# Layer 0's feed-forward network on one Trainium2 core: products by Strassen's scheme in PSUM, and the down projection as a phase of its own

## The chip, the core and the metric

The kernel runs on one core of a Trainium2 chip. Its engines work side by side, each through a queue of its own: TensorE (PE, matrix products into the accumulators of PSUM), VectorE (DVE), ScalarE (ACT), GpSimd (POOL), and SyncE (SP), which here issues nearly all transfers from and to memory. The metric is the device time of one execution in microseconds (us). Lower is better.

## The reference, cut to what matters

Two layers (`DEPTH = 2`) work on 512 tokens `x` and, in layer 0, 256 context tokens `h` as well. D_MODEL is 1024, D_FF is 2816.

```python
for l in range(DEPTH):
    ctx_out = l < DEPTH - 1
    mod_x = jnp.split(sc_x @ w_mod[l] + b_mod[l], 6, axis=-1)
    ...
    mx, mc = token_mixers(ux, uc, w_in[l], ...)      # four branches, gates, w_out
    x = x + mod_x[2] * rmsnorm(mx, norm_g[l, 1])
    fx = conv_ffn(modulate(rmsnorm(x, norm_g[l, 2]), mod_x[3], mod_x[4]), ffn_up[l], ffn_conv[l], ffn_down[l])
    x = x + mod_x[5] * rmsnorm(fx, norm_g[l, 3])
    if ctx_out:
        ...

def conv_ffn(u, w_up, w_conv, w_down):
    a = dwconv3(u @ w_up, w_conv)                    # a filter of three taps along the tokens
    gate, val = jnp.split(a, 2, axis=-1)
    return (jax.nn.silu(gate) * val) @ w_down
```

`token_mixers` has an mLSTM, a pooling, a window attention and a short convolution. Each one's output goes through a projection, is weighted with a sigmoid gate, and the four are added ("merge") ahead of `w_out`. The attention's softmax has one more logit per head, the sink.

## The kernel before, in words

**Numbers.** A product of fp32 matrices is made from three products of rounded parts: weight hi by token hi, weight hi by token lo, weight lo by token hi. A weight block (K 1024 x 128 columns, 512 KB) is loaded by SP into a `raw` slot, ACT rounds it to `wh` (L255), and POOL makes `wl = raw - wh` in the slot of `raw` (L256). Slots go round in a fixed ring: 5 of `raw`, 3 of `wh`, more of `raw` in layer 1. The tokens are held as `UH` and `UL`, 8 blocks of 128 features by 768 tokens (512 x, 256 context; layer 1 has 512).

**Order.** The code builds a program which a scheduler then orders for each engine. `run((a, ra), (b, rb))` interleaves generators at the given rates. Every engine runs its instructions in its order, and waits for a semaphore where an operand is not there yet.

**FFN of layer 0.** The 2816 hidden columns are 22 pairs of a gate block and a value block, 128 columns each. `up_pair(f)` makes 2 x 48 matmuls of 384 tokens (8 blocks x 3 passes x 2 halves of the tokens, L301) into a ring of three PSUM tiles `mm, mm, b2`. Then come the filter (`dwconv`: ACT L561, DVE L563 and L566), Silu (ACT L1304), gate times value, and the split into `ah`, `al`. Pairs are taken in groups (`EDGES`), and after a group `down` (L1317) multiplies its activations, which stay in SBUF, with rows of `ffn_down` for six token tiles of 128 and adds the result to `y` (L1343 and after). The last group's `down` is followed, tile by tile, by `residual` (L541 to L556: norm, gain, residual, norm) and `to_u` (L521 to L527: transposes, modulation, new `UH`, `UL` for layer 1).

**Beside it** runs `mod_dve(1, ch)` for six channels: layer 1's modulation, a product of one row with 1024 x 1024 weights. DVE makes it from `mraw` tiles (512 KB each, two buffers) with 32 multiply-adds of 512 columns (L427) a channel where both x and context need it (channels 1 and 0), 16 elsewhere.

**Elsewhere.** In a merge, the product (`mm`) times `bth` goes to SBUF (DVE L1026) and is added to `acc` (L1027). After the last merge ACT L1254 and DVE L1255 split `acc` into `UH` and `UL` for the `w_out` products (L1270). In the attention each softmax has scores (PE L750, L754), mask and maximum (L761), exp with its sum `den` (ACT L767), the sink's exp (ACT L769), their sum (DVE L770), the reciprocal (L771) and the scaling (L772); transposes follow (L795), and products with the values (L782).

Of the kernel before, what the change touches and what calls it, by code (L numbers as in the profile page):

```python
# [17 lines left out]
P = 128  # L18
# [6 lines left out]
EDGES = ((0, 3, 6, 9, 12, 15, 17, 22), (0, 4, 8, 12, 15, 18, 22))  # L25
DOWN_ROWS = (5, 4)
DOWN_AHEAD = (2, 1)
# [17 lines left out]
def block_kernel(  # L45
# [148 lines left out]
    ps_ = {"mm": 2, "b2": 1, "b1": 2, "pool": tc.alloc_tile_pool(name="psum", bufs=1, space=PSUM)}  # L194

    def pst(tag, w):
        return ps_["pool"].tile([P, w], F32, tag=tag, name=nm(tag), bufs=ps_[tag])
# [209 lines left out]
    def mod_dve(l, ch, md):  # L407
# [104 lines left out]
    def to_u(np_, l, which, j0, xns, ks=range(KC)):  # L512
# [5 lines left out]
        for k in ks:  # L518
            ps = b1()
            for i, xn in enumerate(xns):  # L520
                PE.transpose(ps[:, i * P : (i + 1) * P], xn[:, k * P : (k + 1) * P], ident)  # L521
            tt = np_.tile([P, n], F32, tag="tt", name=nm("tt"), bufs=3)
            ACT.activation(
                tt, ps[:, 0:n], AF.Identity, scale=a[:, k, part : part + 1], bias=b[:, k, part : part + 1]
            )
            DVE.tensor_copy(UH[:, k, o : o + n], tt)  # L526
            DVE.tensor_sub(UL[:, k, o : o + n], tt, UH[:, k, o : o + n].bitcast(F32))  # L527
            yield
# [155 lines left out]
    def attention(l, ap, pools, kept, ys, pc, sk, mid):  # L684
# [37 lines left out]
        for jq in range(4):  # L722
# [10 lines left out]
            for i in range(6 if hc else 4):  # L733
                pt = bp.tile([P, 2, 640], F32, tag="pt", name=nm("pt"), bufs=2)
# [8 lines left out]
                w = len(kts) * P  # L743
                for hd in range(2):
                    h = 2 * jq + hd
# [25 lines left out]
                    DVE.reciprocal(den, den)  # L771
                    DVE.tensor_scalar(pt[:, hd, 0:w], pt[:, hd, 0:w], den, None, op0=ALU.mult)  # L772
                    if next(av_part, 0) is None:
                        yield
                def finish(i=i, jq=jq, g=g, kts=kts, pt=pt):
# [3 lines left out]
                    def times(k0, kk, ph, pl):  # L779
                        for a, kt in enumerate(kk):  # L780
                            for r in (ph, pl):
# [204 lines left out]
    def gate_tile(l, nb, f, p, stops=()):  # L986
# [4 lines left out]
        th = p.tile([P, T], F32, tag="th", name=nm("bth"), bufs=2 if l == 0 else 4)  # L991
# [14 lines left out]
    def merge(l, nb, ys, acc, ct, first, kept):  # L1006
        hc = l == 0
        n = T if hc else TX
        yh, yl = ({p: y and y[q] for p, y in ys.items()} for q in range(2))
        for f in range(8):  # L1010
            if kept:
                th = ct.tile([P, T], F32, tag="th", name=nm("bth"), bufs=2 if hc else 4)
# [8 lines left out]
            pb = wide(mm(), hc)  # L1021
            proj(pb, bw[0], bw[1], yh, yl, 4, lambda i: i * 256 + ff * P, even(hc))
            if first:
                DVE.scalar_tensor_tensor(acc[f][:, 0:n], th[:, 0:n], 1.0, pb[:, 0:n], op0=ALU.add, op1=ALU.mult)
# [24 lines left out]
    def pool_branch(l, ys, pc, ct):  # L1049
# [3 lines left out]
        for g in range(4):  # L1053
# [17 lines left out]
            iv = ct.tile([P, T], F32, tag="th", name=nm("iv"), bufs=2 if hc else 4)  # L1071
            nc.sync.dma_start(iv, k_pinv[g].partition_broadcast(P))
# [38 lines left out]


# [363 lines left out]
```

## Time and profile before

| | |
|---|---|
| three runs, median (lowest to highest) | 2670.55 us (2669.33 to 2674.66) |
| the profiled execution: device time | 2671.79 us |
| its span in the trace | 2670.1 us |
| mean granted TensorE clock | 0.992 of full speed |
| moved over the span | 297.96 MB, mean 112 GB/s |
| layer 0 FFN in the span, from its first products to layer 1's first | 1020.09 to 1600.67 us |

The span is what the trace covers, from the first instruction to the last. Busy time of PE counts overlapping matmuls, so a difference between starts of equal matmuls is the better measure of what one takes. In the rows below `L301` is a line of the kernel, `out<-in` are names of the program, `x16` is a count, and `[1.17 <-ACT wh L255]` is idle time ahead of the first instruction of a group and what ended it. "PEld" is TensorE's loading of weights, which lies beside its products.

### The profile page before, as it was taken

Reading aid. Unit: us, or ns where it says so; the run is one execution under the profiler, and the core shown is the slowest. Engines: PE = TensorE matmul, PEld = TensorE weight load, DVE = VectorE, ACT = ScalarE, POOL = GpSimd, SP = SyncE. Lnnn points to the kernel's source line nnn. Section 1 sums busy time; section 2 is a strip of 40 time slices with the busy share of each in tenths; the row PEclk is TensorE's granted clock in tenths of the full one; section 3 lists DMA queues with packets and bytes.
Section 4 is the critical chain, followed back from the end, with each engine's and each line's share of the span. In section 5 each row is a group of like instructions: output and inputs, shape, how many; then the busy total and the mean of one; then the engine's idle time right before and its main releaser. Section 6 shows DMA issues by size and latency. Waiting matters only on the chain. (4 is left out here: it accounts for less than half of the span.)

```text
span 2670.1 us, 35624 instructions
## 1 busy us (share of the span) xinstructions
PE 2577.0 (97%) x13859; PEld 2302.0 (86%) x13859; DVE 1444.8 (54%) x2510; ACT 991.5 (37%) x1663; POOL 896.8 (34%) x522
## 2 busy tenths in 40 slices
PE   6999999999999999999999999999999999999998
PEld 2988999999999979989999978778888877888886
DVE  6688784333462546577656565665434636523334
ACT  3454553222222334323322345555232333543332
POOL 3222223333232323333332333323343443444432
PEclk9999999999999999999999999999999999999999
DMA  6334353322332433233433342323433436433321
GB/s 231 91 111 127 109 158 122 108 80 64 102 93 65 135 128 120 87 110 119 134 121 101 126 136 80 111 81 117 127 106 98 121 96 189 150 95 95 101 64 56
DMA packets 321267, 297.96 MB, mean 112 GB/s; under 512 B 12532, under 2 KB 264252, under 8 KB 321100
## 3 DMA queue, kind: packets, MB, share of 16 engines
q1 hardware_dynamic: 320184, 294.11, 35.9%
q8 instruction: 110, 1.80, 0.3%
q10 hardware_dynamic: 916, 1.58, 0.2%
q14 instruction: 57, 0.47, 0.1%
HBM read 269.30 MB, written 26.35 MB: 111 GB/s over the span
## 5 line engine op out<-in xcount | busy, mean ns | idle before, releaser
L256 POOL TENSOR_TENSOR wl<-raw,wh 128x1024 fp32r<-128x1024 f32 x260 | 636.9, 2452 | 1189.7 <-ACT wh L255 1150.3
L301 PE MATMUL mm<-UH,wh 128*128 128x384 f32 (+2 forms) x2248 | 652.1, 350 | 8.5 <-DVE UH L526 4.8
L301 PE MATMUL mm<-UL,wh 128*128 128x384 f32 (+2 forms) x2248 | 642.4, 347 | 1.8 <-DVE UL L527 1.8
L255 ACT CAST wh<-raw 128x1024 fp32r<-128x1024 f32 x260 | 272.8, 1050 | 535.7 <-PE mm L301 359.8
L301 PE MATMUL mm<-UH,wl 128*128 128x384 f32 (+2 forms) x2248 | 449.1, 346 | 0.0
L301 PEld LDWEIGHTS mm<-UH,wh 128*128 128x128 f32 x2248 | 409.3, 189 | 31.7 <-DVE UH L526 5.7
L301 PEld LDWEIGHTS mm<-UL,wh 128*128 128x128 f32 x2248 | 411.9, 189 | 22.5 <-DVE UL L527 2.2
L301 PEld LDWEIGHTS mm<-UH,wl 128*128 128x128 f32 x2248 | 392.2, 188 | 21.3 <-issue 3.3
L427 DVE SCALAR_TENSOR_TENSOR macc<-mraw,sc,macc 128x512 f32<-128x512 f32 x224 | 204.6, 938 | 20.7 <-DMA mraw<-in_w_mod_dram 19.7
L301 PE MATMUL mm<-ys,wh 128*128 128x384 f32 (+1 forms) x768 | 168.6, 366 | 8.7 <-DVE bth L1026 8.1
L1238 POOL TENSOR_TENSOR wrl<-raw,wrh 128x1024 fp32r<-128x1024 f32 x48 | 119.1, 2494 | 168.9 <-ACT wrh L1237 126.4
L301 PEld LDWEIGHTS mm<-ys,wh 128*128 128x128 f32 x768 | 137.6, 191 | 21.1 <-DVE bth L1026 5.2
L563 DVE SCALAR_TENSOR_TENSOR fcv<-mm,fcol,fcv 128x511 f32<-128x511 f32 x89 | 58.3, 655 | 136.6 <-ACT fcv L561 136.5
L1237 ACT CAST wrh<-raw 128x1024 fp32r<-128x1024 f32 x60 | 62.7, 1051 | 142.7 <-DMA raw<-in_ffn_down_dram 69.2
L301 PE MATMUL mm<-U,wh 128*128 128x512 f32 (+1 forms) x496 | 111.2, 377 | 0.1
L301 PEld LDWEIGHTS mm<-U,wh 128*128 128x128 f32 x496 | 89.2, 188 | 17.2 <-DVE y L545 0.3
L1026 DVE SCALAR_TENSOR_TENSOR bth<-bth,mm 128x768 f32<-128x768 f32 (+1 forms) x48 | 39.2, 818 | 113.6 <-PE mm L301 106.1
L1317 PE MATMUL mm<-wrh,ah 128*128 128x512 f32 x302 | 95.6, 393 | 1.1 <-DVE fcv L566 1.1
L1317 PE MATMUL mm<-wrl,ah 128*128 128x512 f32 x302 | 95.5, 393 | 0.0
L1317 PE MATMUL mm<-wrh,al 128*128 128x512 f32 x302 | 95.5, 393 | 0.0
L301 PE MATMUL mm<-ys,wl 128*128 128x384 f32 (+1 forms) x384 | 86.1, 360 | 0.0
L563 DVE SCALAR_TENSOR_TENSOR cv<-mm,pcol,cv 128x511 f32<-128x511 f32 (+1 forms) x28 | 17.7, 632 | 116.9 <-ACT cv L561 116.9
(306 smaller groups left out, 4138.0 us busy)
## 6 DMA issues: line engine op xcount, KB each, us to landing
raw<-in_w_in_dram SPq DMA_DIRECT2D x140, 512.0 KB
mraw<-in_w_mod_dram SPq DMA_DIRECT2D x88, 512.0 KB
raw<-in_ffn_up_dram SPq DMA_DIRECT2D x88, 512.0 KB
raw<-in_ffn_down_dram SPq DMA_DIRECT2D x44, 512.0 KB
raw<-in_w_branch_dram SPq DMA_DIRECT2D x32, 512.0 KB
gates<-bth SPq DMA_DIRECT2D x24, 384.0 KB
bth<-gates SPq DMA_DIRECT2D x24, 384.0 KB
raw<-in_w_out_dram SPq DMA_DIRECT2D x16, 512.0 KB
```

Of the source, the lines that this page charges most:

```text
L255: ACT.copy(h, raw)
L256: POOL.tensor_sub(lo, raw, h.bitcast(F32))
L301: PE.matmul(ps[:, c0:c1], lhsT=lw, rhs=r, start=s, stop=e)
L427: DVE.scalar_tensor_tensor(acc[v], mr[:, kk], sc[:, k, v : v + 1], acc[v], op0=ALU.mult, op1=ALU.add)
L563: DVE.scalar_tensor_tensor(dst[:, a + 1 : b], src[:, a : b - 1], w[0], dst[:, a + 1 : b], op0=ALU.mult, op1=ALU.add)
L1026: DVE.scalar_tensor_tensor(th[:, 0:n], th[:, 0:n], 1.0, pb[:, 0:n], op0=ALU.add, op1=ALU.mult)
L1237: ACT.copy(h, raw)
L1238: eng.tensor_sub(lo, raw, h.bitcast(F32))
L1317: PE.matmul(ps[:, h], lhsT=av[i][q][:, j * P : (j + 1) * P], rhs=ws[i][r][:, h], start=pi == 0 and i == 0, stop=pi == 2 and i == len(av) - 1,)
```

## The change

**Up products.** The first three pairs (`PLAIN`) stay as they were. Each of the other 19 is a product of a 2 x 2 block matrix of weights (gate and value block by two halves of K, 512 each) with a 2 x 2 block matrix of tokens (two halves of K by two halves of the tokens, 384 each). It is made from 7 block products (Winograd's form of Strassen's scheme) of 12 matmuls in place of 8 of 12. The weights are combined for each pair (`s12` on DVE, `s34` on POOL), the tokens once (`T1` to `T4`). Partial sums stay in PSUM half `v0`, from which ACT takes copies `p1`, `u1`, `u2` as it grows. A pair's last two products (`rest`) come after the next pair's first. Seven `raw` and six `wh` slots are lent for this phase, which make 12 and 9. The activations go to memory (`a_d`, 393 KB a pair), in fp32.

**Down** follows when all pairs are done: two sweeps of three token tiles, each over all 22 pairs, accumulating in three PSUM tiles. Each sweep loads and splits all of `ffn_down` and reads its half of `a_d`. The matmuls of `down` remain as many as before.

**Modulation.** Channels 1 and 0 run beside the sweeps at rate 0.35, channels 2, 4, 3 and 5 beside layer 1's heads at rate 0.4 with one `mraw` buffer in place of two.

**Merges and attention.** The product is weighted and added in its PSUM tile. The last merge uses the ring `mm, mm, b2` and writes `UH`, `UL` itself. The sink is one more column under the exp; the two heads of a tile share a reciprocal.

The diff, cut to its core:

```diff
+PLAIN = 3
+LAST_DOWN = 4
+RATE_MOD1 = 0.4
...
+        def conv_act(f, g, v):
...
+            ACT.activation(g[:, 0:T], cg, AF.Silu)
+            DVE.tensor_mul(cv, g[:, 0:T], cv)
+            nc.sync.dma_start(a_d[f], cv)
...
+        def prepare(f):
...
+            DVE.tensor_add(s12[:, lo], r2[:, lo], r2[:, hi])
+            DVE.tensor_sub(s12[:, hi], s12[:, lo], r1[:, lo])
+            POOL.tensor_sub(s34[:, lo], r1[:, lo], r2[:, lo])
+            POOL.tensor_sub(s34[:, hi], r1[:, hi], s12[:, hi])
+            got = part(r1, o1), part(s12, os12), part(s34, os34)
...
+            ACT.copy(h, r2[:, hi])
+            POOL.tensor_sub(l_, r2[:, hi], h.bitcast(F32))
...
+        for j in range(3):
...
+            DVE.tensor_sub(t1, blocks(j + 3, 0), blocks(j, 0))
...
+        def pair(f, weights):
...
+            product(v0, w1, 0, "11", True, True)
+            ACT.copy(p1, v0)
+            if pend:
+                pend.pop()()
+            product(g0, w1, 512, "21", True, True)
+            product(v0, w12, 512, "T2", False, True)
+            ACT.copy(u1, v0)
+            product(g1, w12, 0, "T1", True, True)
+            product(v0, w34, 0, "T3", False, True)
+            ACT.copy(u2, v0)
+            DVE.tensor_add(v1, g1, u2)
+            def rest():
+                product(v0, w22, 0, "T4", False, True)
+                product(g1, w34, 512, "22", False, True)
+                DVE.tensor_add(g0, g0, p1)
+                DVE.tensor_add(g1, g1, u1)
+                conv_act(f, g, v)
...
+        def factors(s, f):
+            w = split(load(ffn_down[0][f * P : (f + 1) * P, :].unsqueeze(1), 1))
...
+            nc.sync.dma_start(af, a_d[f, :, s * HT : (s + 1) * HT])
+            ACT.copy(ah, af)
+            (DVE, POOL)[f % 2].tensor_sub(al, af, ah.bitcast(F32))
...
+        run((sweeps(), 1), (seq(*[mod_dve(1, ch, mp) for ch in (1, 0)]), 0.35))
...
-                DVE.scalar_tensor_tensor(th[:, 0:n], th[:, 0:n], 1.0, pb[:, 0:n], op0=ALU.add, op1=ALU.mult)
-                DVE.tensor_add(acc[f][:, 0:n], acc[f][:, 0:n], th[:, 0:n])
+                DVE.scalar_tensor_tensor(pb, th[:, 0:n], 1.0, pb, op0=ALU.add, op1=ALU.mult)
+                DVE.tensor_add(pb if last else acc[f][:, 0:n], acc[f][:, 0:n], pb)
+            if last:
+                ACT.activation(UH[:, f, 0:n], pb, AF.Copy, scale=0.5)
...
-                    es = small("es", 1, 4)
-                    ACT.activation(es, sk[:, h : h + 1], AF.Exp, bias=negm)
-                    DVE.tensor_add(den, den, es)
...
+        mods1 = seq(*[mod_dve(1, ch, dp, 1) for ch in (2, 4, 3, 5)]) if l == 1 else iter(())
+        run((heads(), 1), (fills(), 1), (mods1, RATE_MOD1))
...
-            run((up, 1), (seq(*[mod_dve(1, ch, fp) for ch in (1, 0, 2, 4, 3, 5)]), 1))
```

The order on the engines moves with it, at three places that matter below. First, ScalarE in the middle of the up products. Before, one cast of weights (`wh`) stood between the steps of the filter (`fcv`), the modulation (`mh`) and the activations (`ah`):

```order
L255 CAST wh_2572_11090<-raw_2571_11088 128x1024
L1308 CAST ah_2536_2537_10979<-fcv_2534_2535_10971 128x768
L255 CAST wh_2610_11374<-raw_2609_11372 128x1024
L561 ACTIVATE fcv_2569_2570_11082<-mm_2568_11033,fcol_2016_8329 128x768
L436 CAST mh_2599_11303<-macc_2582_2583_11165 128x512
L1304 ACTIVATE fcv_2569_2570_11082<-fcv_2569_2570_11082 128x768
L255 CAST wh_2626_11450<-raw_2625_11448 128x1024
```

Now one pair's row of eleven instructions is this, from its copy `u2` to the next pair's `u2`. The tiles `v_2409` and `mm_2408` are of one pair, `v_2433` is the next one's; `raw_2445` is the value block of the pair after those in work:

```order
L1269 COPY u2_2414_2415_10563<-v_2409_10560 128x384
L1261 COPY p1_2434_2435_10697<-v_2433_10696 128x384
L593 ACTIVATE cv_2440_2441_10739<-v_2409_10560,fcol_1946_8165 128x768
L593 ACTIVATE cg_2442_2443_10745<-mm_2408_10559,fcol_1946_8165 128x768
L1197 CAST wh_2454_10827<-raw_2445_10807 128x512
L1266 COPY u1_2436_2437_10698<-v_2433_10696 128x384
L1179 CAST wh_2450_10819<-s12_2446_10809 128x1024
L1179 CAST wh_2452_10823<-s34_2447_10810 128x1024
L1171 ACTIVATE mm_2408_10559<-cg_2442_2443_10745 128x768
L1179 CAST wh_2472_10951<-raw_2468_10941 128x1024
L1269 COPY u2_2438_2439_10699<-v_2433_10696 128x384
```

Three casts of 1024 columns and one of 512 stand between copies that PE's next products need, where two stood for a pair before.

Second, GpSimd at the same place: of one pair, `s34` in two halves (L1193, L1194), and the low parts of its four weights:

```order
L1193 TENSOR_TENSOR s34_2447_10810<-raw_2444_10805,raw_2445_10807 128x512
L1198 TENSOR_TENSOR wl_2455_10828<-raw_2445_10807,wh_2454_10827 128x512
L1194 TENSOR_TENSOR s34_2447_10810<-raw_2444_10805,s12_2446_10809 128x512
L1180 TENSOR_TENSOR wl_2449_10816<-raw_2444_10805,wh_2448_10815 128x1024
L1180 TENSOR_TENSOR wl_2451_10820<-s12_2446_10809,wh_2450_10819 128x1024
L1180 TENSOR_TENSOR wl_2453_10824<-s34_2447_10810,wh_2452_10823 128x1024
```

Before, there were two of 1024 columns for a pair (L256) and the down weights' (L1238). Three of 512 were added, and one of 1024.

Third, TensorE where the products of `up` end and those of `down` begin. Before, each group of pairs was followed by its `down` with weights `wrh`, `wrl` and activations `ah`, `al` from SBUF:

```order
L301 MATMUL mm_2363_9879<-UL_3_59,wh_2361_9875 128x384 x2
L301 MATMUL mm_2363_9879<-UH_2_58,wl_2362_9876 128x384 x16
L1317 MATMUL b2_2378_9954<-wrh_2340_2341_9796,ah_2307_2308_9589 128x512 x2
L1317 MATMUL b2_2378_9954<-wrl_2342_2343_9797,ah_2307_2308_9589 128x512 x2
L1317 MATMUL b2_2378_9954<-wrh_2340_2341_9796,al_2309_2310_9590 128x512 x2
```

Now it happens once, behind the last pair's last product, and `ah_2688` comes from memory:

```order
L1244 MATMUL mm_2660_12029<-UL_3_59,wh_2644_11911 128x384
L1244 MATMUL mm_2660_12029<-UH_2_58,wl_2645_11912 128x384 x4
L1312 MATMUL mm_2681_12188<-wh_2685_12193,ah_2688_12198 128x512 x2
L1312 MATMUL mm_2681_12188<-wl_2686_12194,ah_2688_12198 128x512 x2
L1312 MATMUL mm_2681_12188<-wh_2685_12193,al_2689_12199 128x512 x2
```

The first two `ah` lie in space that held `UH` and `UL` (`spare` in the code), which the product ahead of them still reads.

## Rows read from the trace of the kernel before

**Rows 1.** Page: each engine's busy us, share of the span, instructions.

```profile
PE 2577.0 (97%) x13859; PEld 2302.0 (86%) x13859; DVE 1444.8 (54%) x2510; ACT 991.5 (37%) x1663; POOL 896.8 (34%) x522
```

**Rows 2.** Windows: stretch, length, busy us of PE PEld DVE ACT POOL, clock, DMA share, GB/s.

```profile
0.00:50.00 50.00, 32.36 (x92) 12.95 (x93) 32.73 (x49) 15.34 (x23) 12.81 (x25) 0.93 0.89 298
943.00:951.00 8.00, 4.24 (x13) 3.17 (x12) 7.45 (x10) 1.43 (x4) 2.78 (x2) 0.79 0.57 172
1049.00:1550.00 501.00, 497.13 (x2679) 464.48 (x2678) 309.11 (x368) 154.00 (x182) 177.79 (x78) 1.00 0.37 115
1890.00:2150.00 260.00, 255.89 (x1325) 220.92 (x1324) 127.00 (x264) 81.22 (x124) 103.33 (x62) 1.00 0.39 113
2215.00:2250.00 35.00, 30.09 (x110) 23.30 (x110) 33.16 (x37) 14.85 (x25) 17.05 (x8) 0.85 0.76 227
```

**Rows 3.** Timeline of PE: first products of two neighbouring blocks of columns.

```profile
1049.14 0.52 PE L301 MATMUL mm<-UH,wh 128*128 128x384 f32 x2
...
1057.47 0.51 PE L301 MATMUL mm<-UH,wh 128*128 128x384 f32 x2
```

**Rows 4.** Chain that ended last: 24 matmuls of 512 columns in `down`.

```profile
2359.30 5.48 PE b L1317 x24
```

**Rows 5.** ScalarE's groups by line and form: busy, mean ns, idle before.

```profile
L255 ACT CAST wh<-raw 128x1024 fp32r<-128x1024 f32 x260 | 272.8, 1050 | 535.7 <-PE mm L301 359.8 <-issue 81.5 <-DMA raw<-in_ffn_up_dram 47.8
L1304 ACT ACTIVATE fcv<-fcv 128x768 f32<-128x768 f32 x22 | 18.6, 843 | 25.3 <-DVE fcv L566 25.3
L811 ACT COPY avl<-b 64x256 f32<-64x256 f32 x40 | 14.8, 369 | 22.4 <-PE b L782 21.7
L1058 ACT COPY pd<-mm 128x512 f32<-128x512 f32 x8 | 4.7, 585 | 9.2 <-PE mm L301 8.5 <-DVE hb L959 0.8
```

**Rows 6.** VectorE's groups by line and form.

```profile
L427 DVE SCALAR_TENSOR_TENSOR macc<-mraw,sc,macc 128x512 f32<-128x512 f32 x224 | 204.6, 938 | 20.7 <-DMA mraw<-in_w_mod_dram 19.7
L545 DVE TENSOR_TENSOR y<-y,gt 128x512 f32<-128x512 f32 x20 | 13.3, 688 | 8.1 <-ACT sq L503 4.9 <-DMA gt<-gdram 3.2
L902 DVE TENSOR_TENSOR E<-b,E 128x384 f32<-128x384 f32 x24 | 12.0, 551 | 9.0 <-PE b L892 9.0
```

**Rows 7.** GpSimd's groups by line and form.

```profile
L256 POOL TENSOR_TENSOR wl<-raw,wh 128x1024 fp32r<-128x1024 f32 x260 | 636.9, 2452 | 1189.7 <-ACT wh L255 1150.3 <-issue 23.5 <-DVE den L771 8.9
L437 POOL TENSOR_TENSOR ml<-macc,mh 128x512 fp32r<-128x512 f32 x32 | 41.6, 1313 | 103.5 <-ACT mh L436 86.6 <-DVE yr L814 9.7 <-DVE pt L772 5.2
```

**Rows 8.** Timeline: three loads of 512 KB tiles, issue and first use.

```profile
1068.87 5.80 SPq L262 DMA_DIRECT2D raw<-in_ffn_up_dram  x3
...
1074.35 1.04 ACT L255 CAST wh<-raw 128x1024 fp32r<-128x1024 f32 x1 [6.45 <-DMA raw<-in_ffn_up_dram]
...
1117.60 2.52 SPq L415 DMA_DIRECT2D mraw<-in_w_mod_dram  x2
...
1121.22 0.75 DVE L427 SCALAR_TENSOR_TENSOR macc<-mraw,sc,macc 128x512 f32<-128x512 f32 x1 [1.49 <-DMA mraw<-in_w_mod_dram]
...
1204.55 0.34 SPq L262 DMA_DIRECT2D raw<-in_ffn_down_dram  x1
...
1208.62 1.05 ACT L1237 CAST wrh<-raw 128x1024 fp32r<-128x1024 f32 x1 [3.16 <-DMA raw<-in_ffn_down_dram]
```

**Rows 9.** Timeline, 1209.5 to 1210.5: GpSimd and VectorE side by side.

```profile
1209.75 2.39 POOL L1238 TENSOR_TENSOR wrl<-raw,wrh 128x1024 fp32r<-128x1024 f32 x1 [4.28 <-ACT wrh L1237]
...
1210.31 2.38 DVE L427 SCALAR_TENSOR_TENSOR macc<-mraw,sc,macc 128x512 f32<-128x512 f32 x1
```

**Rows 10.** Timeline of PE where the two layers' last merges end.

```profile
947.23 1.22 PE L1270 MATMUL mm<-wrh,UH 128*128 128x512 f32 x2 [3.76 <-DVE bth L1026]
...
2240.19 1.12 PE L301 MATMUL mm<-ys,wh 128*128 128x512 f32 x3 [2.12 <-DVE bth L1026]
```

**Rows 11.** Waits of PE: total us, times, longest us.

```profile
PE b L521 <- ACT y L555: 9.3, 5, 2.6
...
PE b L782 <- DVE pl L804: 4.5, 4, 1.8
```

More of the change, by code (lines that the diff above doesn't have):

```diff
@@ L192, in more_slots, with __init__, back, psum @@
             slots["raw"].append(arena.base + 4 * arena.take(1024)[0])
-    ps_ = {"mm": 2, "b2": 1, "b1": 2, "pool": tc.alloc_tile_pool(name="psum", bufs=1, space=PSUM)}
+    class Lent:
+        def __init__(self, **counts):
+            self.got = []
+            for kind, n in counts.items():
+                for _ in range(n):
+                    piece = arena.take(1024)
+                    off = arena.base + 4 * piece[0]
+                    slots[kind].insert(0, off)
+                    self.got.append((kind, off, piece))
+        def back(self):
+            for kind, off, piece in self.got:
+                slots[kind].remove(off)
+                arena.give(*piece)
+    cuts = []
+    def psum(**tags):
+        cuts.append((tags, tc.alloc_tile_pool(name=nm("psum"), bufs=1, space=PSUM)))
+    psum(mm=2)
+    psum(b2=1, b1=2)
     def pst(tag, w):
-        return ps_["pool"].tile([P, w], F32, tag=tag, name=nm(tag), bufs=ps_[tag])
+        tags, pl = next(c for c in cuts if tag in c[0])
+        return pl.tile([P, w], F32, tag=tag, name=nm(tag), bufs=tags[tag])
     def mm():
@@ L1004, in early_gates, with merge @@
                 yield
-    def merge(l, nb, ys, acc, ct, first, kept):
+    def merge(l, nb, ys, acc, ct, first, kept, last=False):
         hc = l == 0
+        places = cycle((mm, mm, b2) if last else (mm,))
         n = T if hc else TX
@@ L1113, in xsrc, with make_rows, rows @@
+    def make_rows():
+        def rows(wr, w, k, bufs, eng=POOL):
+            raw, _ = load(w[k * P : (k + 1) * P, :].unsqueeze(1), 1)
+            h = wr.tile([P, 1024], F32R, tag="wrh", name=nm("wrh"), bufs=bufs)
+            lo = wr.tile([P, 1024], F32R, tag="wrl", name=nm("wrl"), bufs=bufs)
+            ACT.copy(h, raw)
+            eng.tensor_sub(lo, raw, h.bitcast(F32))
+            return h, lo
+        return rows
     def xsrc(l, j):
@@ L1231, in block_kernel @@
         wr = Pool()
-        def rows(wr, w, k, bufs, eng=POOL):
-            raw, _ = load(w[k * P : (k + 1) * P, :].unsqueeze(1), 1)
-            h = wr.tile([P, 1024], F32R, tag="wrh", name=nm("wrh"), bufs=bufs)
-            lo = wr.tile([P, 1024], F32R, tag="wrl", name=nm("wrl"), bufs=bufs)
-            ACT.copy(h, raw)
-            eng.tensor_sub(lo, raw, h.bitcast(F32))
-            return h, lo
+        rows = make_rows()
         fc = conv_params(l)
         ws = []
-        for k, _ in enumerate(merge(l, 0, y4, acc, mg, False, True)):
+        if not hc:
+            UH, UL = (at("U1", [P, KC, TX], F32R, base + 4 * KC * TX * i) for i in range(2))
+            arena.give(-(RAW + WH) * 1024 - 2 * KC * TC, 2 * KC * TC)
+        for k, _ in enumerate(merge(l, 0, y4, acc, mg, False, True, True)):
             if k < 6:
@@ L1347, in ffn @@
             ffn.last = (pairs[lo:hi], ws)
-        if l == 0:
-            pcs[1] = params(1, nc.sync)
-            up = ffn()
-            for _ in range(2):
-                next(up)
-            run((up, 1), (seq(*[mod_dve(1, ch, fp) for ch in (1, 0, 2, 4, 3, 5)]), 1))
-        else:
-            run((ffn(), 1))
+        run((ffn(), 1))
         fp.release()
```

276 lines of the change are left out of this document (215 added, 61 removed).

## The prediction

> **What bounds the kernel now.** The page's first part comes first [rows 1]: TensorE is busy for 97% of the span, every other engine for little more than half of it or less. The windows then say whether this holds where the change is made [rows 2]: over 501 us in the middle of layer 0's feed-forward network (FFN) PE is busy for 497.1 us at the full granted clock (1.00), while DVE has 309 us of work, ACT 154 and POOL 178, and the transfers run at 115 GB/s. So this stage lasts as long as its matmuls do, and fewer matmuls shorten it, if nothing else becomes as long. PE's timeline prices them: two neighbouring blocks of 48 matmuls of 384 columns start at 1049.14 and 1057.47 [rows 3], so one takes 8.33 / 48 = 0.1735 us and a block product of 12 takes 2.08. A matmul of 512 columns in `down` takes 5.48 / 24 = 0.228 us [rows 4].
>
> What has to be found out is whether the other engines keep pace with 7 products a pair (84 x 0.1735 = 14.57 us, before 96 x 0.1735 = 16.66), and what the new order costs at its seams.
>
> **A, the products.** 19 pairs x 12 matmuls x 0.1735 = -39.6 us. `down` keeps its 22 x 6 x 3 x 2 = 792 matmuls, 792 x 0.228 = 181 us, before and after.
>
> **B, the ring of one pair.** By sums the other engines have room in 14.57 us. ACT: three casts of 1.05, one of half the width, Silu 0.84, two filter steps of Silu's width and three copies of 0.48 [rows 5], some 8 us. POOL: three of 2.45 and three of 1.31 [rows 7], 11.3 us. But the order closes a ring. `v0` is one accumulator: each copy of it (`u1`, `u2`) must be done before the next product adds to it. ACT's row in the order shows `u2` behind the casts of weights for a later pair, and these wait for a load into the slot that product T4 of the pair in work sets free (12 `raw` slots, four a pair, so three pairs round). Followed once round: T4 2.08; load, the mean of two lone ones, 3.62 and 4.07 [rows 8], 3.85; POOL's first half of `s34` 1.31 (512 columns, as L437 [rows 7]); DVE's first half of `s12` 0.69 (as L545 [rows 6]); ACT's half cast 0.59 (as L1058, 512 columns [rows 5]); POOL's low part of it 1.31 and second half of `s34` 1.31; ACT's cast of `s34` 1.05, Silu 0.84, the next cast 1.05 [rows 5]; `u2` 0.48 (384 columns, between 0.369 for 256 and 0.585 for 512 [rows 5]); DVE's add of `v1` 0.55 (as L902 [rows 6]); then T4 again. The sum is 15.11 us. A hand-over between engines takes some 0.08 us (a cast that starts at 1208.62 and lasts 1.05 is followed by POOL at 1209.75 [rows 8, 9]), and eight of them would add 0.6, though ends on one engine overlap the next start. I take 15.3, so B = 19 x (15.3 - 14.57) = +14. From below it is 0 (the ring has slack). From above the load takes 5.5 us, as behind two others [rows 8], the ring 16.8 to 16.95, and B = +45.
>
> In that ring DVE's `s12` starts only when POOL's `s34` has ended, although neither needs the other. I put it so because the trace has such a case: a DVE multiply-add that begins at 1210.31 beside a POOL subtraction (1209.75, 2.39 us) lasts 2.38 us [rows 9], where the mean is 0.94 [rows 6]. Without the hold `s12` lies beside `s34`, the sum is 14.42, below PE's 14.57, and B falls to 0 or a little more.
>
> The Trainium skill (page "SBUF — State Buffer", section "Who interferes with whom") makes this a rule that speaks against the change: a VectorE instruction with two inputs in SBUF and a GpSimd one that reads SBUF share a pair of ports, and the later one stands still until the earlier has ended. By it the ring is as I have put it, without it the phase would come out 14 us shorter. The trace agrees in the case named.
>
> **C, the start of the phase, +6 (2 to 14).** The first copies `p1` stand behind POOL's two halves of `s34` and a cast: 2 x 1.31 + 1.05 + 0.48 = 4.15 us, of which one product covers 2.08, so 2.1 are left. While three pairs run plainly, the ring of PSUM has two tiles in place of three (the rest goes to `v`), so a product waits for the filter of the one two before: four steps of 768 columns on ACT and DVE, some 3.4 us at Silu's 0.84 each [rows 5] (an estimate), part of it covered. The 12 subtractions that make T1 to T4 are 12 x 0.69 = 8.3 us of DVE between the filters of these pairs; hidden, or all of it open: that is the upper end.
>
> **D, from up to down, +5 (2 to 10).** The first `ah` lie in space of `UH` and `UL`, so their load can start only when the last product has read it, and PE waits for a load (3.62 [rows 8]) and a cast (0.48): 4.1 us. When PE last waited that long, at 947, the clock granted over those 8 us was 0.79 in the mean [rows 2, 10]; as much again costs 8 x 0.21 = 1.7. The load is of 197 KB in place of 512 and may land sooner.
>
> **E, the end of the layer, -4 (-8 to +3).** Before, transposes in the tail waited 9.3 us in five waits for the normalised `y` [rows 11]. Now three of the six tiles are finished a sweep earlier, and only the last two waits stay. Against it stands the change of sweeps: the same three PSUM tiles are read by ACT and DVE before the second sweep writes them.
>
> **F, merges, -4 (-9 to +3).** `w_out` waits 3.76 us at 947 behind the last merge and its pass over `acc`, with 1.7 us of clock, and PE waits 2.12 at 2240 [rows 2, 10]. DVE's and ACT's pass now lies inside the merge, over three PSUM tiles in turn. The last block's chain (two DVE steps, ACT, DVE) stays open. In the window from 2215 DVE is busy 33.2 of 35 us [rows 2], so work saved there shows.
>
> **G, attention, -3 (-8 to +3).** One ACT and one DVE instruction less per head and tile, and all high products ahead of the low ones: the waits for `pl` were 4.5 us in four [rows 11]. The first head's scaling now waits for the second.
>
> **H, modulation in layer 1, +3 (0 to +10).** 64 multiply-adds x 0.938 = 60 us of DVE [rows 6] go into about 260 us in which DVE is busy for 127 and PE idle for 4.1 [rows 2]. There is room, but DVE's order can hold a mask or a filter behind a modulation step that waits for its load: with one buffer each of 32 loads is waited for, 1.49 us where two buffers did it before [rows 8], 48 us in all if none of it is covered (the scenario below).
>
> **I, the sweeps themselves, +4 (0 to +15).** For each f PE has 18 matmuls, 4.1 us. POOL has 2.45 and half of the activations' low parts, about 2.9. DVE has 60 us of modulation in 181. Transfers: 44 x (524 + 197 KB) + 16 x 524 KB = 40.1 MB in about 185 us, 217 GB/s. POOL and DVE together would have 130 + 60 + 12 = 202 us if they never overlapped; where they hold each other as in [rows 9], this is the term that grows.
>
> **Sum:** -39.6 + 14 + 6 + 5 - 4 - 4 - 3 + 3 + 4 = -18.6. The profiled execution has a span of 2670.1, and 2671.79 as device time, 1.7 around it; the median of the runs is 1.2 lower than that. So 2670.1 - 18.6 + 1.7 - 1.2 = 2652 us.
>
> **The rivals.** A difference under 0.2% (5.3 us) is about what a measurement of this kernel cannot tell from none.
>
> 1. *As summed:* 2652, its own range 2638 to 2664 (B from 0.3 to 1.2 us a pair, the seams at either half of their bounds). Chance 0.62.
> 2. *PE alone sets the pace of the pairs* (no hold on `s12`, or a load in under 3.5 us): B = 0, and -32.6 in all, 2638. The rows that speak for it are 3.62 as a landing at 512 KB, and that the sum is only 0.5 us over PE's; against it is the hold in [rows 9]. With quiet seams it reaches 2628. Chance 0.16.
> 3. *Loads land late:* where a load comes behind the write of `a_d` and another load, 5.5 us [rows 8], the ring is 16.8, as long as the old pair, B = +43, 2681. For it: at 1068 three loads queue so. Against: in the order each load of the ring stands alone behind a write that has been ready for long. Chance 0.08.
> 4. *The other side, down becomes bound by transfers:* the sweeps want 217 GB/s where this stage had 115 [rows 2]. At 157 GB/s, 40.1 MB would take 255 us in place of 188: +67, 2719. It decides below about 200 GB/s. Against it the trace shows 298 GB/s in the first 50 us and 227 from 2215 on, with the DMA engines busy 0.89 and 0.76 [rows 2]. Chance 0.05.
> 5. *Modulation holds DVE in layer 1:* the 48 us of H uncovered in place of 3: 2697. Against it: with two buffers, such loads held DVE for 19.7 us over all 224 steps of the kernel [rows 6]. Chance 0.05.
>
> The remaining 0.04 is a mixture of late seams that ends within 5 us of before. Faster by over 0.2%, below 2665: nearly all of 1, all of 2 and part of the rest, 0.80. Slower: 3, 4, 5 with less than all of their price at times, 0.14. The range of 8 in 10 takes 1 with both of its flanks and 2: 2630 to 2670.
>
> **What would show it.** In the changed profile: starts of the first product of successive pairs 15.3 us apart (14.6 means rival 2, 16.8 rival 3); idle time of PE before T4, ended by DVE `v1`, of about 0.7 us a pair; DVE's `s12` starting as POOL's `s34` ends, or lasting 1.3 us and more; one wait of about 4 us before the first `down` product, and a clock under 1.0 behind it; the sweeps at 4.1 us for each f with a rate near 215 GB/s (6 us and 150 GB/s means rival 4); layer 1 as long as before within 5 us. The prediction is wrong if the pairs are at 14.6 and the seams add nothing, or if PE waits in the sweeps for weights (`wl`) that POOL has not split in time.

## The result, and the profile after

The changed kernel takes 2702.7 us (median of five runs, 2699.3 to 2708.1) against 2670.7 before: a ratio of 1.0119, 95% interval 1.0105 to 1.0134, slower by some 32 us. Forecast were 2652 us, 2630 to 2670. The profiled execution is the longest of the five, with 2708.07 us and a span of 2706.3.

The page's first part, to be read beside [rows 1]: TensorE is busy for 10 us less, GpSimd for 207 us more, and the span is 36.2 us longer. TensorE's 228 matmuls fewer are 39.6 us at 0.1735 us each, so some 30 us of that gain went into products that took longer (the granted clock was 0.982 in the mean, 0.992 before), and its idle time grew from 93 to 139 us. Waits are paid twice here, as idle time and as a slower clock behind it: after the wait of 3.2 us ahead of `down`, the granted clock was 0.50 of full speed from 1382.0 to 1387.3.

```profile
PE 2567.0 (95%) x13631; PEld 2280.4 (84%) x13631; DVE 1445.6 (53%) x2478; ACT 1053.1 (39%) x1696; POOL 1104.0 (41%) x644
```

Four windows of the changed kernel, cut at events that both traces have: three plain pairs, 19 pairs of the scheme, the two sweeps of `down`, and layer 1 from its first gates to its `w_out`. Columns as in [rows 2].

```profile
1015.47:1082.68 67.21, 57.81 (x378) 57.11 (x377) 42.14 (x63) 33.24 (x43) 43.02 (x21) 0.92 0.21 64
1082.68:1382.01 299.33, 282.60 (x1598) 275.94 (x1597) 165.51 (x262) 140.52 (x190) 207.79 (x109) 1.00 0.34 109
1382.01:1601.46 219.45, 200.43 (x842) 158.88 (x843) 133.02 (x133) 84.07 (x141) 145.13 (x89) 0.94 0.56 186
1679.38:2279.32 599.94, 568.41 (x2871) 474.95 (x2871) 348.51 (x666) 230.28 (x389) 216.01 (x114) 0.98 0.46 137
```

The stretch of layer 1 in the kernel before, between the same two events, is a row of its own:

```profile
1670.16:2244.64 574.48, 555.77 (x2821) 468.89 (x2821) 306.53 (x633) 229.17 (x412) 209.53 (x108) 0.99 0.40 117
```

So: up to the FFN's first product the kernel is 4.6 us ahead (1015.47 against 1020.09). From there to layer 1's first gates it takes 663.9 in place of 650.1 us, +13.8. Layer 1 then takes 599.9 in place of 574.5, +25.5, with 42 us more work on VectorE, and the rest +1.5. The 299.33 - 3.4 = 295.9 us of the scheme (its last product ends 3.4 us ahead of the window's end) are 20.6 less than 19 x 16.66; the three plain pairs take 67.2 where 6 x 8.33 = 50 and some transposes would do; the sweeps take 219 where their products need 181.

Inside the scheme, the list of TensorE's waits from 1085 to 1376 and its timeline at two neighbouring pairs:

```profile
PE v L1244 <- DVE v L1270: 11.9, 17, 1.2
```

```profile
1127.78 0.44 PE L1244 MATMUL v<-th,wh 128*128 128x384 f32 x1 [0.66 <-DVE v L1270]
1143.22 0.44 PE L1244 MATMUL v<-th,wh 128*128 128x384 f32 x1 [0.58 <-DVE v L1270]
```

These pairs follow at 15.44 us, and T4 waits for `v1` in 17 of the 19 pairs: the ring of the forecast. The other engines' timeline shows it as written there. VectorE's first half of `s12` starts beside GpSimd's first half of `s34` and lasts 1.46 us, where such a step takes 0.69 [rows 6]; at the end come the cast of `s34` behind POOL, Silu, the next cast, the copy `u2` and the add `v1`.

```profile
1133.91 1.29 POOL L1193 TENSOR_TENSOR s<-raw,raw 128x512 f32<-128x512 f32 x1 [2.76 <-DMA raw<-in_ffn_up_dram]
...
1134.29 1.46 DVE L1191 TENSOR_TENSOR s<-raw 128x512 f32<-128x512 f32 x1
...
1139.46 1.06 ACT L1179 CAST wh<-s 128x1024 fp32r<-128x1024 f32 x1 [1.36 <-POOL s L1194]
...
1140.41 0.81 ACT L1171 ACTIVATE mm<-cg 128x768 f32<-128x768 f32 x1
1141.16 1.04 ACT L1179 CAST wh<-raw 128x1024 fp32r<-128x1024 f32 x1
...
1142.10 0.47 ACT L1269 COPY u<-v 128x384 f32<-128x384 f32 x1
...
1142.60 0.57 DVE L1270 TENSOR_TENSOR v<-mm,u 128x384 f32<-128x384 f32 x1 [0.39 <-ACT u L1269]
```

In the sweeps, VectorE and GpSimd from 1460 on, and then the change of sweeps, where TensorE waits for VectorE's reading of the first PSUM tile (L577), which stands behind two multiply-adds of the modulation:

```profile
1460.90 5.20 POOL L284 TENSOR_TENSOR wl<-raw,wh 128x1024 fp32r<-128x1024 f32 x2
1463.85 9.82 DVE L455 SCALAR_TENSOR_TENSOR macc<-mraw,sc,macc 128x512 f32<-128x512 f32 x4 [2.36 <-DMA mraw<-in_w_mod_dram]
1466.06 1.46 POOL L1306 TENSOR_TENSOR al<-af,ah 128x384 fp32r<-128x384 f32 x1
1467.48 5.64 POOL L284 TENSOR_TENSOR wl<-raw,wh 128x1024 fp32r<-128x1024 f32 x2
...
1487.87 4.26 DVE L455 SCALAR_TENSOR_TENSOR macc<-mraw,sc,macc 128x512 f32<-128x512 f32 x2
...
1492.06 0.68 DVE L577 TENSOR_TENSOR y<-mm,gt 128x512 f32<-128x512 f32 x1
...
1494.24 1.22 PE L1312 MATMUL mm<-wh,ah 128*128 128x512 f32 x2 [4.51 <-DVE y L577]
```

A multiply-add takes 2.45 us at 1463.85, in step with GpSimd's subtractions, where one that nothing holds takes 0.75; the mean of the 56 in the sweeps is 1.30 us. TensorE's waits in the sweeps (1360 to 1600) are for the modulation's two matmuls (L467) and for this change:

```profile
PE b L467 <- ACT mh L464: 8.8, 3, 5.3
PE mm L1312 <- DVE y L577: 5.4, 2, 4.5
PE b L467 <- POOL ml L465: 3.5, 5, 1.0
PE mm L1312 <- ACT ah L1305: 3.2, 1, 3.2
```

The wait for `ah` ends where the sweeps' window begins. The other three and two shorter ones come to the 19 us in which TensorE is idle there. With the clock at 0.94 of full speed over 219 us (13 us) and 50 small matmuls of the modulation and of transposes (some 6 us, an estimate from their columns), they account for the 38 us. In layer 1 (1679 to 2279), VectorE's waits for the modulation's loads:

```profile
DVE macc L455 <- DMA mraw<-in_w_mod_dram: 45.9, 18, 5.3
DVE macc L453 <- DMA mraw<-in_w_mod_dram: 20.9, 6, 7.7
```

### The profile page after: what moved, and what is told of

Its sections match the earlier page's. It is cut to its first block, busy times and chain, and to the rows that moved or that the text cites. A ratio compares the mean times of both kernels' runs of the same rounds, so it can differ in the third digit from the quotient of the medians.

```text
span 2706.3 us, 35636 instructions
## 1 busy us (share of the span) xinstructions
PE 2567.0 (95%) x13631; PEld 2280.4 (84%) x13631; DVE 1445.6 (53%) x2478; ACT 1053.1 (39%) x1696; POOL 1104.0 (41%) x644
## 5 line engine op out<-in xcount | busy, mean ns | idle before, releaser
L329 PE MATMUL mm<-UH,wh 128*128 128x384 f32 (+2 forms) x1848 | 554.8, 356 | 14.4 <-DVE cv L598 8.0
L329 PE MATMUL mm<-UL,wh 128*128 128x384 f32 (+2 forms) x1848 | 545.6, 352 | 1.8 <-DVE UL L559 1.8
L329 PE MATMUL mm<-UH,wl 128*128 128x384 f32 (+2 forms) x1848 | 377.0, 350 | 0.0
L329 PEld LDWEIGHTS mm<-UH,wh 128*128 128x128 f32 x1848 | 341.3, 191 | 36.9 <-issue 10.5
L329 PEld LDWEIGHTS mm<-UL,wh 128*128 128x128 f32 x1848 | 343.4, 191 | 23.1 <-DVE UL L559 2.2
L329 PEld LDWEIGHTS mm<-UH,wl 128*128 128x128 f32 x1848 | 324.6, 189 | 21.2 <-issue 2.8
L1244 PE MATMUL v<-th,wh 128*128 128x384 f32 x228 | 78.5, 344 | 13.5 <-DVE v L1270 11.9
L1180 POOL TENSOR_TENSOR wl<-s,wh 128x1024 fp32r<-128x1024 f32 x38 | 90.0, 2395 | 0.0
L1244 PE MATMUL v<-tl,wh 128*128 128x384 f32 x228 | 76.4, 335 | 0.0
L802 ACT ACTIVATE pt<-pt,negm 128x513 f32<-128x513 f32 (+2 forms) x80 | 58.1, 727 | 33.9 <-DVE negm L799 33.4
```

The costliest lines, as they stand in the source:

```text
L329: PE.matmul(ps[:, c0:c1], lhsT=lw, rhs=r, start=s, stop=e)
L802: ACT.activation(pt[:, hd, 0 : w + 1], pt[:, hd, 0 : w + 1], AF.Exp, bias=negm, accum_out=den[:, hd : hd + 1])
L1180: POOL.tensor_sub(lo, src, h.bitcast(F32))
L1244: PE.matmul(ps, lhsT=w[r][:, o + k * P : o + (k + 1) * P], rhs=B[b][q][:, k], start=start and i == 0, stop=stop and i == 11, skip_group_ch ...
```

## The experiments

Theory: the 50 us that the forecast missed are VectorE's, which stands still in three places (in layer 1 for loads into one buffer; in the sweeps, and where the pairs of the scheme are made, behind GpSimd), with work in its order that TensorE waits for. Rivals: transfers bound the sweeps; the edits of attention and merges cost the time in layer 1; the block products don't pay. All ratios are to the kernel before on the same chip; times behind them are (ratio - 1.0119) x 2671 us, against the changed kernel. Each ratio is known to some 0.15 to 0.3%, so a difference of two carries about 6 us either way, more for plain22.

**1. Less modulation in layer 1** (l1_mods_short):

```diff
-            for k2 in range(4):
+            for k2 in range(1 if l == 1 and ch >= 2 else 4):
```

> It leaves out three quarters of the modulation that was moved into layer 1 (channels 2, 4, 3, 5: 8 loads and 16 multiply-adds in place of 32 and 64). In the changed kernel the stretch from the first gate waits of layer 1 to its w_out products is some 26 us longer than before, and VectorE waits 55 us there for the modulation's loads. Theory: those steps stand in VectorE's order ahead of what TensorE needs, so 18 to 28 us come back, 2675 to 2685 us. Rival: the edits of attention and merges, or the new order of layer 1, cost the time; then it stays at 2698 to 2704.

Measured: 1.0047 (1.0032 to 1.0061), -19 us, with three quarters of these steps and loads left out. The theory's number. From the first gates to `w_out` layer 1 now takes 579.6 us (1678.93 to 2258.49), 5 more than before and with a quarter of the steps still there, so the attention and the merges are not to blame.

**2. Less modulation in the sweeps** (sweep_mods_short; the same edit with `ch < 2`):

> It leaves out three quarters of the modulation beside the down sweeps (channels 1 and 0). In the changed kernel TensorE waits 12 us there for the cast behind the modulation and 4.5 for its low part, 5 to 6 for the change of sweeps, and the clock falls behind some of these waits. Theory: VectorE's multiply-adds stand behind GpSimd's subtractions (2.45 us each in place of 0.7), and TensorE and the change of sweeps wait for them; 14 to 24 us come back, 2679 to 2689 us. Rival: the sweeps are held by transfers, 40 MB in some 220 us; with 6 MB less, 3 to 6 us come back, all of them as shorter waits for loads.

Measured: 1.0052 (1.0034 to 1.0071), -18 us, as the theory had it. But the change of sweeps still waits 4.5 us, behind the steps that are left. What went is in the other waits (for `mh` 1.1 us in place of 8.8, for `ml` 1.0 in place of 3.5) and in the clock, 0.97 in place of 0.94.

**3. Its loads alone** (sweep_one_load):

```diff
-                mr = md.tile([P, 2, 512], F32, tag="mraw", name=nm("mraw"), bufs=bufs)
+                if k2 == 0 or l == 0 or ch >= 2:
+                    mr = md.tile([P, 2, 512], F32, tag="mraw", name=nm("mraw"), bufs=bufs)
                 nc.sync.dma_start(
...
-                )
+                ) if k2 == 0 or l == 0 or ch >= 2 else None
```

> It leaves out three quarters of the modulation's loads in the sweeps (12 of 16, 6 of 40 MB); all eight multiply-adds of a half channel read its first tile, so every step on VectorE stays. Theory: the steps held by GpSimd cost the 16 us that the short version gave, not their loads; 0 to 5 us come back, 2697 to 2703 us. Rival: transfers, or SyncE's row that stands behind these loads, cost them; 10 to 16 us come back, 2687 to 2693 us.

Measured: 1.0118 (1.0101 to 1.0134), 0 us. Transfers don't bound the sweeps, and what the short version gave came mostly from the steps. The loads are not quite free in the trace: TensorE's wait for `mh` falls from 8.8 to 1.3 us, but the wait at the change of sweeps grows from 5.4 to 10.2, with steps that GpSimd holds ahead of it, so one wait took the place of another. In the profiled execution the sweeps are 6 us shorter, which the times of the runs don't show.

**4. The same in layer 1** (l1_one_load; as 3 with `ch < 2`):

> It leaves out three quarters of the loads of the modulation in layer 1 (channels 2, 4, 3, 5): all eight multiply-adds of a half channel read its first tile. All of VectorE's steps stay. Theory: the wait for a load into the one buffer is what costs, 55 us of VectorE's time in all; most of the 20 us that the short version gave come back, 2683 to 2690 us. Rival: the multiply-adds themselves (0.75 us, up to 2.5 where GpSimd holds them) cost; then no more than 5 us come back, 2697 us or more.

Measured: 1.0081 (1.0066 to 1.0096), -10 us. Between the two: about half of the 19 us is waiting for loads. VectorE's waits for them fall from 66.8 to 20.1 us, so only a fifth or so of that waiting had reached the time.

**5. s34 on VectorE** (s34_on_dve):

```diff
-            POOL.tensor_sub(s34[:, lo], r1[:, lo], r2[:, lo])
-            POOL.tensor_sub(s34[:, hi], r1[:, hi], s12[:, hi])
+            DVE.tensor_sub(s34[:, lo], r1[:, lo], r2[:, lo])
+            DVE.tensor_sub(s34[:, hi], r1[:, hi], s12[:, hi])
```

> Both halves of s34 on VectorE, nothing left out. Theory: the pairs follow each other at 15.5 us because of the ring load, s34, s12, casts, Silu, copy, T4; without GpSimd's 2.6 us in it and with one hold less the pairs come at 14.6 to 14.9 us, 12 to 18 us for 19 pairs, 2685 to 2691 us. Rival: VectorE and GpSimd together are the bound (each holds the other); then more two-input steps on VectorE leave the pairs at 15.5 us or make them longer, 2700 us or more.

Measured: 1.0054 (1.0035 to 1.0072), -17 us. From 1085 to 1360 TensorE now has one wait, where it had 18, 16 of them for `v1`:

```profile
PE v L1244 <- DVE v L1270: 1.2, 1, 1.2
```

The pairs now come at 14.7 us (from 1091.0 to 1355.2 for 19 adds of `v1`). The ring is confirmed, by moving the two steps that made it longer than TensorE's own 14.57 us.

**6. No block scheme** (plain22: `PLAIN = 22`, T1 to T4 not made, three PSUM tiles in turn):

> All 22 pairs as plain products, no block scheme, no sums; the rest of the change stays. Theory: the scheme is worth 19 x (16.66 - 15.52) = 22 us less its own start (waits of 7 us and clock), so 10 to 22 us are lost, 2713 to 2725 us. Rival: its start and its hold on the other engines eat all of it; then 2698 to 2706 us.

Measured: 1.0107 (1.0078 to 1.0135), -3 us, which the intervals do not tell from none. My theory fell: the scheme gained nothing in this kernel. The profile shows where 20.6 us went: from the FFN's first product to the first `down` the plain version needs 1390.1 - 1012.9 = 377 us, the changed one 366.5, so the start kept ten of them; and from there to layer 1's gates 281 against 297 us, where 16 of the 64 modulation steps had been done beside the plain pairs already. That this is why is read from the trace, and no run varies it alone.

**7. PSUM at the start** (start_free; Silu of the plain pairs in SBUF, tiles `mm, mm, b2` in turn):

> The three plain pairs write their Silu to SBUF, so that their PSUM tiles come free after the filter, and use three PSUM tiles in turn; nothing is left out. Theory: the waits of 4.9 and 2.4 us behind the filter, and the clock of 0.92 over 62 us (5 us), come from there; 7 to 12 us less, 2690 to 2696 us. Rival: VectorE is busy with T1 to T4 there and the filter stays late; 2699 us or more.

Measured: 1.0122 (1.0107 to 1.0137), +1 us. The PSUM tiles alone are not it. In the changed kernel's timeline the filter's next step (1046.80) is behind an `s12` step that lasts 3.35 us beside GpSimd's low parts of T2 and T4:

```profile
1039.40 10.77 POOL L1229 TENSOR_TENSOR tl<-tl,th 128x1536 fp32r<-128x1536 f32 x2 [13.18 <-ACT th L1228]
...
1042.87 0.75 DVE L595 SCALAR_TENSOR_TENSOR cg<-mm,fcol,cg 128x511 f32<-128x511 f32 x1
1043.53 3.35 DVE L1192 TENSOR_TENSOR s<-s,raw 128x512 f32<-128x512 f32 x1
1046.80 0.74 DVE L598 SCALAR_TENSOR_TENSOR cg<-mm,fcol,cg 128x511 f32<-128x511 f32 x1
...
1050.56 0.98 PE L329 MATMUL mm<-UH,wh 128*128 128x384 f32 x2 [4.92 <-DVE cv L598]
```

**8. That step on GpSimd** (start_s12_pool):

```diff
+            E = POOL if f < PLAIN + 2 else DVE
+            E.tensor_add(s12[:, lo], r2[:, lo], r2[:, hi])
+            E.tensor_sub(s12[:, hi], s12[:, lo], r1[:, lo])
```

> For the first two pairs of the scheme s12 is made on GpSimd, behind its own subtractions, in place of VectorE; nothing is left out. Theory: in the changed kernel the filter of the first plain pair stands on VectorE behind an s12 step that GpSimd holds for 3.35 us; the wait of 4.9 us and the slow clock behind it go, 4 to 8 us less, 2694 to 2699 us. Rival: the filter is late anyway, or GpSimd's longer row delays the first pairs of the scheme; 2701 us or more.

Measured: 1.0119 (1.0096 to 1.0141), 0 us. The wait of 4.89 us stays. Now VectorE's own low parts of T1 and T3, ahead of the filter, take 6.75 us in place of 3.5:

```profile
1035.90 6.75 DVE L1230 TENSOR_TENSOR tl<-tl,th 128x1536 fp32r<-128x1536 f32 x2
1042.58 0.74 DVE L595 SCALAR_TENSOR_TENSOR cg<-mm,fcol,cg 128x511 f32<-128x511 f32 x1
...
1047.50 0.98 PE L329 MATMUL mm<-UH,wh 128*128 128x384 f32 x2 [4.89 <-DVE cv L598]
```

That the hold stands ahead of the filter is seen in both traces; that it costs the start its 13 us is not shown. The plain version of 6 makes no T's and no sums, and TensorE waits nearly as long at the same place, there for the Silu that writes into the PSUM tile:

```profile
1045.92 0.98 PE L329 MATMUL mm<-UH,wh 128*128 128x384 f32 x2 [4.41 <-ACT mm L1171]
```

Its first six blocks of columns take some 60 us, 6 more than before (54) and 7 fewer than in the changed kernel. As far as these runs show there are two causes, each enough for a wait of 4 to 5 us: 7 took away the Silu in PSUM (4.2 us of wait were left), 6 the sums (4.4 left), and no run both.

**9. GpSimd's subtractions in the sweeps, half and whole** (sweep_wl_dve, sweep_wl_all; the low parts of every second row of `ffn_down`, or all of them, on VectorE):

```diff
-            w = split(load(ffn_down[0][f * P : (f + 1) * P, :].unsqueeze(1), 1))
...
+            ACT.copy(w[0], raw)
+            (POOL, DVE)[f % 2].tensor_sub(w[1], raw, w[0].bitcast(F32))
```

> In the sweeps the low part of every second row of ffn_down is made on VectorE (some 1.3 us) in place of GpSimd (2.45 us); nothing is left out. Theory: VectorE's modulation stands behind GpSimd's subtractions; with half as many of them the multiply-adds fall from 2.4 towards 1 us and TensorE's waits for the modulation and for the change of sweeps shrink, 6 to 14 us less, 2689 to 2697 us. Rival: transfers bound the sweeps; 2700 to 2705 us. Second rival: VectorE becomes the one that TensorE waits for, now for weights; slower than 2705 us.

> In the sweeps the low parts of all rows of ffn_down are made on VectorE; nothing is left out. Theory: without GpSimd's 2.45 us steps nothing holds VectorE's modulation; half of the rows gave 8.6 us, all of them give 14 to 20 us, 2683 to 2689 us. Rival: VectorE then has 44 x 1.3 + 45 + 12 = 114 us and TensorE waits for weights in its order; 2694 us or more.

Measured: 1.0086 (1.0069 to 1.0103), -9 us, as expected, and 1.0094 (1.0071 to 1.0116), -7 us, where the theory wanted 14 to 20. The hold is real, but it is not all of the 18 us. VectorE gets the subtractions in place of the hold, and in the whole version TensorE waits 8.4 us at the change of sweeps (4.5 in the changed kernel), where VectorE's order stands 5.6 us at a load of the modulation.

**10. Modulation beside the attention** (l1_split; channels 2 and 4 there, two buffers):

> Of the four channels in layer 1, two (2, 4) run beside its attention with two buffers at the rate that layer 0 has there, two (3, 5) stay beside the heads with one; nothing is left out. Theory: with two buffers the loads are covered, and GpSimd holds VectorE less there (46 of 146 us busy), so about half of the 20 us comes back: 6 to 13 us, 2690 to 2697 us. Rival: the attention, where VectorE is busy for 88 of 146 us, becomes longer by as much; 2699 us or more.

Measured: 1.0158 (1.0141 to 1.0175), +10 us. The rival: in that stage TensorE now waits 7.0 us in two places for VectorE's X (L762) where it was 2.4, and 4.2 for the softmax's `pt` where it was 0.3. VectorE's idle share there was not free, as its order sets when these are done.

**11. All three at once, work left out** (all_short):

> s34 on VectorE, and three quarters of all six modulation channels of layer 1 left out, in the sweeps and beside the heads. Theory: the three losses lie in three stretches and add up, 17 + 16 + 20 = 53 us: 2646 to 2654 us, some 20 us under the kernel before with most of its modulation left out; so the block products would keep about half of their 40 us even so. Rival: the losses are one chain seen three times; 2665 us or more.

Measured: 0.9911 (0.9896 to 0.9926), -56 us, against 19 + 18 + 17 = 54. The losses add up: three stretches, not one chain.

**12. Nothing left out** (combo2: edits 5, 9 whole and 10; combo3: 5 and 9 whole; combo5: 5 and 9 half, with half tiles in layer 1; combo4: 5 and 9 whole, with half tiles; the half tiles are the edit below, where `bufs == 1` is layer 1 beside the heads):

```diff
...
+            w = 1 if bufs == 1 else 2
+            for k2 in range(8 // w):
+                mr = md.tile([P, w, 512], F32, tag="mraw", name=nm("mraw"), bufs=2)
...
```

> Nothing left out: s34 on VectorE, all low parts of ffn_down in the sweeps on VectorE, and two of the channels of layer 1 beside its attention. Theory: 17 + 9 to 13 + 6 to 13 us come back, 2660 to 2670 us, about even with the kernel before and behind the merges and the attention alone (2660). Rival: the low parts on VectorE put TensorE behind it in the sweeps; 2675 us or more.

> s34 and all low parts of ffn_down in the sweeps on VectorE; modulation where the change put it; nothing left out. Theory: 17 + 14 to 20 us come back, 2664 to 2672 us, even with the kernel before. Rival: 2676 us or more, if VectorE becomes the bound in the sweeps.

> As the kernel with s34 and all low parts of ffn_down on VectorE, and in layer 1 the modulation loads half tiles (256 KB) into two buffers in the space of the one; nothing left out. Theory: with a load under way while the last is used, 4 to 10 us of the 10 that the loads cost come back against that kernel, 2656 to 2665 us. Rival: 64 loads in place of 32 hold SyncE's row; even or slower than that kernel.

> s34 on VectorE, every second low part of ffn_down in the sweeps on VectorE, half tiles in two buffers in layer 1; nothing left out. Theory: half of the low parts gave 8.8 us alone and all of them 6.7; ratio 0.993 to 0.996. Rival: with s34 moved GpSimd's hold in the sweeps is the larger loss; 0.998 or more.

Measured: combo2 1.0014 (1.0001 to 1.0027), combo3 1.0000 (0.9986 to 1.0014), combo4 0.9950 (0.9934 to 0.9966), combo5 0.9976 (0.9965 to 0.9988). Combo2 and combo3 are slower than expected (medians of 2677.6 and 2672.8 us), combo4 is as expected (2660.2), combo5 lies between its theory and its rival. From combo3 to combo4 the half tiles give 13 us, about what the loads cost in 4: VectorE's waits for them in layer 1 are 34.6 us in 21, with twice as many loads, where the changed kernel had 66.8 in 24 and combo3 58.2 in 24.

```profile
DVE macc L456 <- DMA mraw<-in_w_mod_dram: 34.6, 21, 3.4
```

**13. The scheme again** (plain22_combo: combo4 with 22 plain pairs):

> All 22 pairs plain, all low parts of ffn_down in the sweeps on VectorE, half tiles in two buffers in layer 1; no step of the reference left out. It differs from the fastest version so far (ratio 0.995) by the block scheme alone. Theory: at 14.6 us a pair the scheme saves 40 us of products and loses some 20 to 25 at its start and by a sweep that has more left to do; plain is 10 to 20 us slower than that version, ratio 0.999 to 1.0025. Rival: the scheme pays nothing even so; ratio 0.994 to 0.997.

Measured: 1.0050 (1.0032 to 1.0067). Against combo4's 0.9950 the scheme is worth 27 us of its 40, more than I expected, once it runs at TensorE's pace (14.7 us a pair in combo4).

**14. Merges and attention alone, on the kernel before** (before_merge_att):

> The kernel before with the edits of merges and attention alone; feed-forward network and modulation as before. Theory: the last merges' waits of 3.8 and 2.1 us with their slow clock are shorter, and the attention is even; 4 to 10 us less than before, 2662 to 2668 us. Rival: the longer chain at the end of a merge or the later scaling in the softmax eats it; 2670 us or more.

Measured: 0.9957 (0.9940 to 0.9973), 2659.6 us. With nothing left out, this version, combo4 and combo5 beat both kernels, and this one and combo4 are even. But combo4 has these two edits in it as well: the large part of the change, mended as far as here, is worth 2 us beside them, which is within the noise. By 13 the block scheme is worth 27 us, so what comes with it (`down` as a phase of its own and the modulation moved) takes about 25 (1.0050 against 0.9957).

## Why the prediction was wrong

**The ring (B) and the seam (D) were right.** B was +14 at 15.3 us a pair; the pairs came at 15.4, and the whole stretch, with its first waits, has 295.9 - 19 x 14.57 = +19. D was +5; TensorE waited 3.22 us and the next twelve products ran at the slower clock. The choice of the hold for B, from one case in [rows 9], was right: `s12` lasted 1.46 us at 1134.29, and the median of the 19 is 1.54. With D, the slower clock cost 2.6 us (0.50 over 5.3 us), where 1.7 was put.

**H failed.** "Modulation in layer 1, +3" was the step, with 48 us set aside as rival 5 at 0.05. Measured by 1, three quarters of it cost 19. Room by sums (60 us of steps into a stretch with 133 us of idle VectorE) was the wrong test. The steps stand in VectorE's order between others that TensorE waits for, and 24 of the 32 loads into the only buffer stopped that order for 2.8 us in the mean and 7.7 at most. By 4, some 10 us of these stops reached the time; the rest of the 19 came with the steps. The bare 48 us of rival 5 would give 2697, near the measured time, but that is luck: its mechanism gave less than half of the miss. The rows had this: 1.49 us a load with two buffers [rows 8] against 3.62 from issue to landing, so one buffer costs VectorE up to 3.6 - 1.5 more for each.

**I failed.** "+4 (0 to +15)" with the sentence that POOL and DVE would have 202 us if they never overlapped. The stage took 219. The 64 modulation steps, put at 60 us, kept VectorE for 82 (70.1 for the 56 below and 12.2 for the other eight), as a held step counts as busy. By 2, three quarters of them cost 18 us.

```profile
L455 DVE SCALAR_TENSOR_TENSOR macc<-mraw,sc,macc 128x512 f32<-128x512 f32 x56 | 70.1, 1304 | 7.3 <-DMA mraw<-in_w_mod_dram 7.3
```

The sum of 202 against 181 would have been the better forecast; I wrote it down as a bound. By 9, about half of the 18 comes back when the hold goes and VectorE has the subtractions to make itself; how much is the hold's alone is not shown. Rival 4, transfers, is refuted by 3 (its price is 255 - 185 = 70, not 67, which changes nothing). PE never waited in the sweeps for `wl`, and the pairs were not at 14.6 us: neither sign of being wrong that the forecast named was seen.

**C was mis-sized:** +6, measured 67.2 - 54 (the before kernel's time for these columns, by 1020.09 and [rows 3]) = +13. It is at the upper end that I gave. The PSUM tile, as forecast, and VectorE's filter behind the sums are both causes, and how much is each one's stays open (6, 7, 8).

**E, F, G:** F's and G's -7 were right within their ranges: the two edits alone give -11 us (14), in the changed kernel seen as the 4.6 us up to the FFN; in layer 1 H hides what they give. E's -4 was lost in the change of sweeps, which waits 4.5 us; E named that wait and put no price on it.

Over the forecast, B has +5, C +7, H +16 and I +14 (H and I as measured for three quarters of their steps), 42 of the 50 us. The rest is put to E and to the last quarter of H and I; no run shows it. C and I have one thing in common: I priced VectorE's and GpSimd's instructions each by itself where the order put them side by side. H is another: its multiply-adds took 0.99 us in the mean (0.94 in the forecast), so there it was the order and the loads, not the hold. The rule of the Trainium skill that I weighed for B (page "SBUF — State Buffer", section "Who interferes with whom") holds in C and I too; the trace shows it at 1043.53, 1463.85 and 1487.87, and I used it for one term alone.

## What to carry to other kernels

Where VectorE and GpSimd hold each other, as in these sweeps, add their work as if it were one engine's, hold the sum against the length of the stage, and see that no held step stands ahead of one that TensorE waits for. Idle share is no room when an engine works in order; ask what stands behind each added step, and what stops it (one buffer, a load, a hold). And a change of several parts is best timed in parts: here two small edits alone gave 11 us, and the large part took away more than that until its losses were mended.

## What the runs showed of the hardware that was not expected

A VectorE step with one input in SBUF and none in PSUM was held as well: in the sweeps `macc = mraw x sc` (L453, 512 columns) took 1.56 us in the mean of eight, where the median of all 32 in the trace is 0.49. Steps that read PSUM and one SBUF tile did not change beside GpSimd: L577 took 0.68 us at 1492.06 beside a subtraction of GpSimd's, and 0.68 to 0.69 in all 14 such; L1270 took 0.57 in all 19. GpSimd is held too, it seems: its two subtractions of 1536 columns at 1039.40 took 10.8 us together, with VectorE's steps beside them, where 1024 columns take 2.45 (two of 1536 would take some 7.4, an estimate in proportion).

```profile
L453 DVE TENSOR_SCALAR macc<-mraw,sc 128x512 f32<-128x512 f32 x8 | 12.2, 1561 | 4.4 <-DMA mraw<-in_w_mod_dram 4.4
```
